# Split weights of the feed-forward stage in idle big tiles, and adding loads at other places

## The chip, the cores and the metric

The kernel runs on one core of a Trainium2 chip. The metric is the device time of one execution in microseconds (us). Three runs of the kernel before gave 1895.63, 1897.59 and 1898.46 us; their median is 1897.59.

## The reference

One layer of a decoder trunk for 256 tokens, model width 2048, all in 32-bit floats: three parallel mixers, then a gated feed-forward stage, then a per-layer embedding, and a final norm. The change lies in the feed-forward stage (D_FF = 5632).

```python
merged = (jax.nn.sigmoid(m_a) * u_a + jax.nn.sigmoid(m_b) * u_b
          + jax.nn.sigmoid(m_c) * u_c)
x = x + merged @ w_o[i]
h = rms_norm(x, g_ffn[i])
gate, up = jnp.split(h @ w_gate_up[i], 2, axis=-1)
x = x + (jax.nn.silu(gate) * up) @ w_down[i]
x = x + (p[i] @ w_ple[i]) * jax.nn.sigmoid(rms_norm(x, g_ple[i]) @ w_ple_gate[i])
return rms_norm(x, g_final)
```

## The kernel before

TensorE multiplies 32-bit data as a sum of three products of rounded parts. Each weight W is split into whi, W rounded to TensorE's 32-bit input format, and wlo = W - whi; the activations are split too. `three` (L242 to L246) issues the three matmuls, 128x128 by 128x512 each: L244 with whi, L245 with wlo, L246 with whi again.

The feed-forward stage runs from about 1058 us on. Gate and up are made in 11 blocks of 512 columns each (`Quad`, j = 0 to 10), and after the blocks 0 to 2, 3 to 5, 6 to 8 and 9 to 10 come four down groups of 512 output columns each, which use the results of these blocks. Blocks up to the next down groups are called a batch. A block has eight places; each place takes one pair of loads (a gate load and an up load of 512 KB, 128 partitions x 2 x 512) and is of kind "s" or "o" by the string "soosooso". In an "s" pair VectorE also makes sums of the two loads (L236, L276), so that seven products do the work of eight (21 matmuls, with four pieces of split weight). An "o" pair has two pieces and 24 matmuls. A block has 3 x 21 + 5 x 24 = 183 matmuls.

What is done to one load, in order:

- SyncE loads it into one of six raw buffers (L152).
- ScalarE copies it with rounding into whi (L216).
- Then wlo is made in one of two ways. By subtraction: VectorE takes raw - whi (L228). Or by an **adding load**: ScalarE writes -whi into wlo (L220), and a DMA that GpSimd (POOL) issues (L221) fetches the weight once more from memory and adds it there. An adding load takes no time of VectorE and lets the raw buffer go as soon as whi is made.

Before the change the up load of each "o" pair is done with an adding load, five per block; in block 0, which takes the pairs in the order 1, 2, 0, 4, 3, 5, 6, 7, only at places from 4 on (`START`'s second number), which are two "o" pairs, at places 5 and 7. That makes 2 + 10 x 5 = 52.

whi and wlo lie in seven buffers each (`PARTS`), and `room` lets a piece be split only when fewer than seven are in use. A pool of 13 big tiles (128 partitions x 8 x 256 floats) holds the residual stream (two), the split activations (eight) and aT, the transposed results of a batch's blocks (three); a tile for aT is taken when its block's result is transposed, so of the three some are idle until then.

The order of all instructions is fixed when the program is built. `Flow` keeps a model clock for ScalarE and VectorE, with a time for a load to land, a gap between loads, and a time for an adding load; `fill` emits, ahead of each matmul step, the splits and evictions that fit before it by that clock. On the chip each engine takes its queue in this order, and waits for its operands by semaphores. The evictions in question are `quad_mid` (gate part: L1332 on ScalarE, L506 on VectorE), the sigmoids of the result (L1345, ScalarE, with a load of the function table ahead of them), the transposes (L1287 on TensorE) with their copies into aT (L515, L516), and `ev_down` (L506 into xr, on VectorE).

Of the kernel before, what the change touches and what calls it, by code (L numbers as in the profile page):

```python
# [11 lines left out]
F32R = mybir.dt.float32r  # L12
# [7 lines left out]
P = 128  # L20
T = 256
D = 2048
NB = 512
# [17 lines left out]
class Group:  # L41
# [6 lines left out]
    def __init__(self, w, kts, c0, n, stat, evac, need=(), pre=None, kind="tok", cost=1.3, key=None):  # L48
        self.w, self.kts, self.c0, self.n = w, list(kts), c0, n
        self.stat, self.evac, self.need, self.pre, self.kind = stat, evac, need, pre, kind  # L50
        self.cost, self.key = cost, key
        self.ps = None
        self.held = []
# [9 lines left out]
class Quad:  # L63
# [6 lines left out]

    def __init__(self, w, c0, c1, pairs, mid, end, order=None, plain=0):
        self.w, self.cs, self.pairs, self.mid, self.end = w, (c0, c1), pairs, mid, end
        self.order = list(order or range(len(pairs)))
        self.plain = plain
        self.ps = {}


# [14 lines left out]
class Piece:  # L94


    def __init__(self, n):
        self.n = n
        self.ops = []
        self.parts = []  # L100
        self.left = 0
# [12 lines left out]
class Flow:  # L114


    RAWS, PARTS = 6, 7
    LAND, GAP, ADDED = 5.0, 1.3, 8.0

    def __init__(self, nc, tc, pools, nm, big, split, quad_parts):  # L120
# [33 lines left out]

    def room(self, piece):
        self.live = [p for p in self.live if p.left]
        return sum(p.n for p in self.live) + piece.n <= self.PARTS

    def next_split(self):

# [10 lines left out]
    def do_split(self, op):  # L171
        if op.piece is not None and op.piece not in self.live:
            p = op.piece
            for part in ("whi", "wlo"):
                p.parts.append([
                    self.pools["wparts"].tile([P, 2, NB], F32R, tag=part, name=self.nm(part)) for _ in range(p.n)
                ])
            self.live.append(p)
        self.emit(self.todo.pop(0))
        for z in op.frees:  # L180
            z.freed = True
            self.slots.append(op.end)
        self.issue()
# [70 lines left out]
    def add_quad(self, g):  # L254
# [2 lines left out]
        first_p, last_p = g.order[0], g.order[-1]  # L257
        for pos, p in enumerate(g.order):
            kind = g.pairs[p]
            r1, r2 = (Load(g.w, 2 * p, c, NB) for c in g.cs)  # L260
            if kind == "s":
                self.loads += [r2, r1]
                pc = [Piece(1) for _ in range(4)]
                x = []

                def new_sum(x=x):
# [9 lines left out]
                        self.nc.vector.tensor_tensor(out=X(0), in0=R2(0), in1=R2(1), op=ALU.add),  # L276
                    ), [], r2,
                )
                b1 = self.split_ops(pc[0], 0, lambda r=r1: r.raw, load=r1)
                t1 = self.add_op(lambda R2=R2: R2(0), lambda R2=R2: R2(0), lambda R1=R1: R1(0), [t3], r1)  # L280
                t2 = self.add_op(lambda X=X: X(1), lambda R2=R2: R2(0), lambda R2=R2: R2(1), [t1], r1)
                self.split_ops(pc[1], 0, lambda r=r2: r.raw, [t1], r2, [r2])
# [15 lines left out]
                              after=(lambda g=g: self.late(g.mid(g, g.ps), g)) if p == last_s and z == "4" else None)  # L298
            else:
                self.loads += [r2, r1]  # L300
                pc = [Piece(1) for _ in range(2)]
                self.split_ops(pc[1], 0, lambda r=r2: r.raw, load=r2, frees=[r2],
                               neg=None if pos < g.plain else g.w[:, 2 * p : 2 * p + 2, g.cs[1] : g.cs[1] + NB])
                self.split_ops(pc[0], 0, lambda r=r1: r.raw, load=r1, frees=[r1])
# [156 lines left out]
def kernel(  # L461
# [284 lines left out]
    w_in_v, w_gu_v, w_dn_v = wv(w_in), wv(w_gate_up), wv(w_down)  # L746
# [513 lines left out]
    PAIRS = "soosooso"  # L1260
# [163 lines left out]
        return f  # L1424

    NJ = 11
    START = ((1, 2, 0, 4, 3, 5, 6, 7), 4)
    flow.transposes(None, [x_part(3, j) for j in (0, 2)])
    plan = []
    for lo, hi in ((0, 3), (3, 6), (6, 9), (9, NJ)):  # L1430
        for j in range(lo, hi):
            plan.append(Quad(w_gu_v, j * NB, (NJ + j) * NB, PAIRS, quad_mid, quad_end(j), *(START if j == 0 else ())))
        for c in range(4):
            plan.append(Group(w_dn_v, range(4 * lo, 4 * hi), c * NB, NB, blk(aT), ev_down(c, hi == NJ), key="a"))

# [146 lines left out]
```

## Time and profile before

| | us |
|---|---|
| median of three runs | 1897.59 |
| the profiled execution | 1896.41 |
| its span (first to last instruction) | 1894.6 |
| TensorE busy in the span | 1867.9 |
| VectorE busy | 1320.2 |
| ScalarE busy | 1041.1 |
| feed-forward stage's 52 adding loads: median from issue to landing | 8.2 |

The profile is of one execution. Its page gives the busy time of each engine and the costliest groups of instructions; a group's row has the line of the kernel, the engine, the output and inputs by tile, the number of instructions, their busy time and mean in ns, and the idle time ahead of them with what ended it. The timeline gives single instructions: start and duration in us, engine, line, operation, and in brackets the idle time before it and what ended that. Names as in the code: whi and wlo are the split weights, st the split activations, acc an accumulator of TensorE, xr the residual stream, ga, vx and gs the gate's intermediate results. A matmul of 128x512 reads 0.39 us long in a timeline since matmuls overlap; start to start they are 0.227 us apart.

### The profile page before, as it was taken

Reading aid. Unit: us, or ns where it says so; the run is one execution under the profiler, and the core shown is the slowest. Engines: PE = TensorE matmul, PEld = TensorE weight load, DVE = VectorE, ACT = ScalarE, POOL = GpSimd, SP = SyncE. Lnnn points to the kernel's source line nnn. Section 1 sums busy time; section 2 is a strip of 40 time slices with the busy share of each in tenths; the row PEclk is TensorE's granted clock in tenths of the full one; section 3 lists DMA queues with packets and bytes.
Section 4 is the critical chain, followed back from the end, with each engine's and each line's share of the span. In section 5 each row is a group of like instructions: output and inputs, shape, how many; then the busy total and the mean of one; then the engine's idle time right before and its main releaser. Section 6 shows DMA issues by size and latency. Waiting matters only on the chain.

```text
span 1894.6 us, 23186 instructions
## 1 busy us (share of the span) xinstructions
PE 1867.9 (99%) x8589; PEld 1551.7 (82%) x8589; DVE 1320.2 (70%) x1657; ACT 1041.1 (55%) x1204; POOL 71.7 (4%) x74
## 2 busy tenths in 40 slices
PE   8999999999999999999999999999999999999997
PEld 6888888888888888888888778888888888887887
DVE  6457777668888889655556777758765776676654
ACT  6656556554454435644445666546644665465654
POOL 0000000000000000000000011001100110010000
PEclk9999999999999999999999999999999999999999
DMA  8766556556666656676655599679976997698552
GB/s 311 238 181 186 176 177 190 168 154 178 190 186 193 194 160 211 198 236 189 188 189 167 194 255 263 222 199 259 268 228 192 250 263 239 187 252 277 178 161 95
DMA packets 204401, 390.47 MB, mean 206 GB/s; under 512 B 12432, under 2 KB 21264, under 8 KB 203904
## 3 DMA queue, kind: packets, MB, share of 16 engines
q1 hardware_dynamic: 189248, 358.12, 59.5%
q0 software_dynamic: 15040, 30.87, 9.3%
q8 instruction: 67, 1.10, 0.2%
q14 instruction: 46, 0.38, 0.1%
HBM read 386.85 MB, written 2.10 MB: 205 GB/s over the span
## 4 chain that ended last, share of the span: by engine, by line
PE 92%; DMA 3%; DVE 3%; ACT 1%; issue 1%; SPq 0%; DVEq 0%; ACTq 0%
PE acc L651 17%; PE acc L652 17%; PE acc L650 17%; PE acc L246 12%; PE acc L245 12%; PE acc L244 12%; DMA wlo<-in_w_gate_up_dram 1%; DMA raw<-in_w_gate_up_dram 1%; DVE wlo L228 1%; PE tr L719 1%; PE tr L1287 1%; PE sc L928 1%; DMA x<-in_x_feat_dram 0%; DMA pt<-in_p_feat_dram 0%; DVE raw L236 0%
## 5 line engine op out<-in xcount | busy, mean ns | idle before, releaser
L516 DVE TENSOR_TENSOR wlo<-raw,whi 128x1024 fp32r<-128x1024 f32 (+2 forms) x378 | 450.0, 1196 | 293.9 <-ACT whi L515 293.3
L515 ACT ACTIVATE whi<-raw 128x1024 fp32r<-128x1024 f32 (+2 forms) x378 | 391.2, 1037 | 465.1 <-PE acc L652 391.8
L216 ACT ACTIVATE whi<-raw 128x1024 fp32r<-128x1024 f32 (+1 forms) x333 | 332.3, 1006 | 301.4 <-PE acc L246 267.0
L650 PE MATMUL acc<-whi,hhi 128*128 128x512 f32 (+1 forms) x1120 | 432.7, 387 | 5.5 <-ACT whi L515 5.5
L651 PE MATMUL acc<-wlo,hhi 128*128 128x512 f32 (+1 forms) x1120 | 430.1, 384 | 0.5 <-DVE wlo L516 0.5
L652 PE MATMUL acc<-whi,hlo 128*128 128x512 f32 (+1 forms) x1120 | 430.1, 384 | 0.0
L228 DVE TENSOR_TENSOR wlo<-raw,whi 128x1024 fp32r<-128x1024 f32 (+1 forms) x281 | 318.1, 1144 | 155.6 <-ACT whi L216 154.7
L245 PE MATMUL acc<-wlo,st 128*128 128x512 f32 x671 | 262.1, 391 | 4.1 <-DMA wlo<-in_w_gate_up_dram 3.6
L244 PE MATMUL acc<-whi,st 128*128 128x512 f32 x671 | 262.0, 393 | 1.6 <-DVE xr L506 1.5
L246 PE MATMUL acc<-whi,st 128*128 128x512 f32 x671 | 261.5, 391 | 0.0
L650 PEld LDWEIGHTS acc<-whi,hhi 128*128 128x128 f32 x1120 | 210.8, 188 | 46.5 <-ACT whi L515 5.9
L651 PEld LDWEIGHTS acc<-wlo,hhi 128*128 128x128 f32 x1120 | 210.9, 188 | 41.9 <-DVE wlo L516 1.4
L652 PEld LDWEIGHTS acc<-whi,hlo 128*128 128x128 f32 x1120 | 210.7, 188 | 41.3
L245 PEld LDWEIGHTS acc<-wlo,st 128*128 128x128 f32 x671 | 126.3, 188 | 32.0 <-DMA wlo<-in_w_gate_up_dram 5.0
L244 PEld LDWEIGHTS acc<-whi,st 128*128 128x128 f32 x671 | 126.3, 188 | 29.1 <-DVE xr L506 1.5
L246 PEld LDWEIGHTS acc<-whi,st 128*128 128x128 f32 x671 | 126.4, 188 | 26.4
L244 PE MATMUL acc<-whi,aT 128*128 128x512 f32 x352 | 138.3, 393 | 1.5 <-ACT aT L515 1.5
L245 PE MATMUL acc<-wlo,aT 128*128 128x512 f32 x352 | 137.2, 390 | 0.0
L246 PE MATMUL acc<-whi,aT 128*128 128x512 f32 x352 | 136.6, 390 | 0.0
L509 DVE SCALAR_TENSOR_TENSOR cv<-uT,vec,cv 128x255 f32<-128x255 f32 (+15 forms) x240 | 110.8, 466 | 4.8
L221 POOL DMA_DIRECT2D wlo<-in_w_gate_up_dram x52 | 62.6, 1204 | 819.9 <-ACT wlo L220 485.8
L244 PEld LDWEIGHTS acc<-whi,aT 128*128 128x128 f32 x352 | 66.2, 188 | 15.5 <-ACT aT L515 2.1
(276 smaller groups left out, 2073.7 us busy)
## 6 DMA issues: line engine op xcount, KB each, us to landing
raw<-in_w_in_dram SPq DMA_DIRECT2D x262, 512.0 KB, 3.7
raw<-in_w_gate_up_dram SPq DMA_DIRECT2D x176, 512.0 KB, 5.3
raw<-in_w_down_dram SPq DMA_DIRECT2D x88, 512.0 KB, 5.1
wlo<-in_w_gate_up_dram POOLq DMA_DIRECT2D x52, 512.0 KB, 8.2
raw<-in_w_gla_out_dram SPq DMA_DIRECT2D x32, 512.0 KB, 3.6
raw<-in_w_o_dram SPq DMA_DIRECT2D x32, 512.0 KB, 4.0
raw<-in_w_ple_gate_dram SPq DMA_DIRECT2D x24, 512.0 KB, 3.6
raw<-in_w_sc_out_dram SPq DMA_DIRECT2D x16, 512.0 KB, 4.3
```

The source lines that it names most:

```text
L216: a = self._op("A", cost * 0.88, lambda: nc.scalar.activation(out=hi(), in_=src(), func=AF.Copy), deps, load, piece, frees if neg else ())
L221: nc.gpsimd.dma_start(out=lo(), in_=neg, accum_op=ALU.add)
L228: lambda: nc.vector.tensor_tensor(out=lo(), in0=src(), in1=hi().bitcast(F32), op=ALU.subtract),
L244: pe.matmul(o, lhsT=s[0], rhs=w[0], start=start, stop=False)
L245: pe.matmul(o, lhsT=s[0], rhs=w[1], start=False, stop=False)
L246: pe.matmul(o, lhsT=s[1], rhs=w[0], start=False, stop=stop)
L509: dve.scalar_tensor_tensor(out=o, in0=a, scalar=s, in1=b, op0=op0, op1=op1)
L515: a = act.activation(out=hi, in_=src, func=AF.Copy)
L516: b = dve.tensor_tensor(out=lo, in0=src, in1=hi.bitcast(F32), op=ALU.subtract)
L650: pe.matmul(o, lhsT=shi[:, hs], rhs=whi, start=st, stop=False)
L651: pe.matmul(o, lhsT=shi[:, hs], rhs=wlo, start=False, stop=False)
L652: pe.matmul(o, lhsT=slo[:, hs], rhs=whi, start=False, stop=sp)
```

## The change

It has three parts, all in the planning of the gate and up blocks:

- `START`'s second number goes from 4 to 8, so block 0 has no adding load; the up loads at its places 5 and 7 are split by VectorE's subtraction.
- `NEG = (0,)`: in the ten blocks after it the gate load of the "s" pair at place 0 is done with an adding load too: six per block, 60 in all.
- A piece may have a count `may`. Where the seven ordinary buffers are taken, such a piece is split into a big tile instead ("wp": both whi and wlo lie in one), as long as fewer than `may` pieces lie in big tiles. `may` is lo + 3 - j, the number of aT tiles not yet taken when block j's work starts: 3, 2 and 1 in the three blocks of a batch, 3 and 2 in the last batch's two; in the first block of a batch only places from 2 on have it.

```diff
@@ class Flow
     RAWS, PARTS = 6, 7
+    NEG = (0,)
     LAND, GAP, ADDED = 5.0, 1.3, 8.0
...
     def room(self, piece):
         self.live = [p for p in self.live if p.left]
-        return sum(p.n for p in self.live) + piece.n <= self.PARTS
+        return self.held(False) + piece.n <= self.PARTS or self.held(True) < piece.may
+
+    def held(self, extra):
+        return sum(p.n for p in self.live if p.extra == extra)
...
     def do_split(self, op):
         if op.piece is not None and op.piece not in self.live:
             p = op.piece
-            for part in ("whi", "wlo"):
-                p.parts.append([
-                    self.pools["wparts"].tile([P, 2, NB], F32R, tag=part, name=self.nm(part)) for _ in range(p.n)
-                ])
+            p.extra = self.held(False) + p.n > self.PARTS
+            if p.extra:
+                b = self.big("wp", (P, 2, 2, NB), F32R)
+                p.parts = [[b[:, 0, :, :]], [b[:, 1, :, :]]]
+            else:
+                for part in ("whi", "wlo"):
...
             kind = g.pairs[p]
+            may = g.spare if pos > 1 or g.spare < 3 else 0
             r1, r2 = (Load(g.w, 2 * p, c, NB) for c in g.cs)
             if kind == "s":
                 self.loads += [r2, r1]
-                pc = [Piece(1) for _ in range(4)]
+                pc = [Piece(1, may) for _ in range(4)]
...
-                b1 = self.split_ops(pc[0], 0, lambda r=r1: r.raw, load=r1)
+                b1 = self.split_ops(pc[0], 0, lambda r=r1: r.raw, load=r1,
+                                    neg=g.w[:, 2 * p : 2 * p + 2, g.cs[0] : g.cs[0] + NB] if pos in self.NEG and not g.plain else None)
...
-    START = ((1, 2, 0, 4, 3, 5, 6, 7), 4)
+    START = ((1, 2, 0, 4, 3, 5, 6, 7), 8)
...
-            plan.append(Quad(w_gu_v, j * NB, (NJ + j) * NB, PAIRS, quad_mid, quad_end(j), *(START if j == 0 else ())))
+            plan.append(Quad(w_gu_v, j * NB, (NJ + j) * NB, PAIRS, quad_mid, quad_end(j), *(START if j == 0 else (None, 0)), lo + 3 - j))
```

Since the planner's clock sees other costs, the order on the engines moves. All lines of the changed kernel stand 11 to 13 lines lower (L216 is L227, L220 is L231, L221 is L232, L228 is L239, L236 is L247, L276 is L288, L506 is L519, L515 is L528, L1332 is L1345, L1345 is L1358). The first number behind a tile's name is the tile's own.

VectorE in block 0, where place 4's subtractions end, before (wlo_1512, the up load of place 5, isn't there: it is an adding load; wlo_1515 is the gate load's, the next ones belong to place 6):

```order
L228 TENSOR_TENSOR wlo_1515_8547<-raw_1491_8450,whi_1514_8546 128x1024
L236 TENSOR_TENSOR raw_1494_8456<-raw_1494_8456,raw_1499_8470 128x512
L228 TENSOR_TENSOR wlo_1519_8564<-raw_1499_8470,whi_1518_8563 128x1024
L236 TENSOR_TENSOR sum_1517_8561<-raw_1494_8456 128x512
L228 TENSOR_TENSOR wlo_1521_8582<-raw_1494_8456,whi_1520_8581 128x1024
L236 TENSOR_TENSOR raw_1499_8470<-raw_1499_8470,sum_1517_8561 128x512
L228 TENSOR_TENSOR wlo_1524_8601<-sum_1517_8561,whi_1523_8600 128x1024
```

and with the change:

```order
L239 TENSOR_TENSOR wlo_1512_8534<-raw_1485_8435,whi_1511_8533 128x1024
L239 TENSOR_TENSOR wlo_1515_8543<-raw_1491_8450,whi_1514_8542 128x1024
L288 TENSOR_TENSOR sum_1517_8557<-raw_1494_8456 128x512
L239 TENSOR_TENSOR wlo_1519_8560<-raw_1499_8470,whi_1518_8559 128x1024
L247 TENSOR_TENSOR raw_1494_8456<-raw_1494_8456,raw_1499_8470 128x512
L247 TENSOR_TENSOR sum_1517_8557<-raw_1494_8456 128x512
L247 TENSOR_TENSOR raw_1499_8470<-raw_1499_8470,sum_1517_8557 128x512
L239 TENSOR_TENSOR wlo_1521_8581<-raw_1494_8456,whi_1520_8580 128x1024
L239 TENSOR_TENSOR wlo_1524_8594<-sum_1517_8557,whi_1523_8593 128x1024
```

The subtraction of wlo_1512 stands ahead of the rest, which follows behind it; the first sum (L276, now L288), which stood ahead of these rows, comes behind the two subtractions.

ScalarE at the end of block 0 and the start of block 1, before (whi_1535 to whi_1546 belong to place 0 of block 1, whi_1554 and wlo_1555 to the up load of its place 1, ga and gs to block 0's result):

```order
L216 ACTIVATE whi_1535_8640<-raw_1516_8553 128x1024
L216 ACTIVATE whi_1539_8660<-raw_1513_8536 128x1024
L1332 ACTIVATE ga_1538_8658<-acc_1498_8465 128x512
L216 ACTIVATE whi_1543_8698<-sum_1534_8638 128x1024
L216 ACTIVATE whi_1546_8714<-raw_1516_8553 128x512
L216 ACTIVATE whi_1554_8740<-raw_1522_8591 128x1024
L220 ACTIVATE wlo_1555_8741<-whi_1554_8740 128x1024
L1345 ACT_TABLE_LOAD
L1345 ACTIVATE gs_1541_8669<-ga_1538_8658,y_1445_8278 128x512 x2
L216 ACTIVATE whi_1557_8747<-raw_1527_8608 128x1024
```

and with the change (the two rows ahead are whi_1535 and its negated copy, wlo_1536):

```order
L1345 ACTIVATE ga_1541_8664<-acc_1498_8465 128x512
L227 ACTIVATE whi_1537_8651<-raw_1513_8540 128x1024
L227 ACTIVATE whi_1543_8691<-sum_1534_8636 128x1024
L227 ACTIVATE whi_1546_8713<-raw_1516_8549 128x512
L227 ACTIVATE whi_1554_8739<-raw_1522_8584 128x1024
L1358 ACT_TABLE_LOAD
L1358 ACTIVATE gs_1542_8671<-ga_1541_8664,y_1445_8278 128x512 x2
L231 ACTIVATE wlo_1555_8740<-whi_1554_8739 128x1024
L227 ACTIVATE whi_1557_8746<-raw_1527_8613 128x1024
```

The negated copy of wlo_1555, which its adding load waits for, has moved from ahead of the table load and the sigmoids to behind them.

ScalarE where the down groups end and block 6 begins, before (whi_2079 to whi_2088 are place 0 of block 6, whi_2091 the up load of its place 1):

```order
L216 ACTIVATE whi_2079_11336<-raw_2065_11248 128x1024
L216 ACTIVATE whi_2083_11358<-raw_2060_11226 128x1024
L216 ACTIVATE whi_2086_11377<-sum_2078_11322 128x1024
L216 ACTIVATE whi_2088_11393<-raw_2065_11248 128x512
L216 ACTIVATE whi_2091_11411<-raw_2068_11266 128x1024
L220 ACTIVATE wlo_2092_11412<-whi_2091_11411 128x1024
L216 ACTIVATE whi_2094_11430<-raw_2071_11284 128x1024
```

and with the change (whi_2068 to whi_2077 are place 0, whi_2080 is the up load of place 1, the wp tiles belong to place 2):

```order
L231 ACTIVATE wlo_2069_11329<-whi_2068_11328 128x1024
L227 ACTIVATE whi_2072_11351<-raw_2049_11218 128x1024
L227 ACTIVATE whi_2075_11370<-sum_2067_11314 128x1024
L227 ACTIVATE wp_2086_11429<-raw_2063_11294 128x1024
L231 ACTIVATE wp_2086_11429<-wp_2086_11429 128x1024
L227 ACTIVATE whi_2077_11386<-raw_2054_11240 128x512
L227 ACTIVATE whi_2080_11404<-raw_2057_11258 128x1024
L227 ACTIVATE wp_2088_11435<-raw_2066_11312 128x1024
L231 ACTIVATE wlo_2081_11405<-whi_2080_11404 128x1024
L227 ACTIVATE whi_2083_11423<-raw_2060_11276 128x1024
```

The splits of place 2, with a negated copy, stand ahead of the last split of place 0 and of place 1's own.

More of the change, by code (lines that the diff above doesn't have):

```diff
@@ L63, with __init__ @@
 class Quad:
-    def __init__(self, w, c0, c1, pairs, mid, end, order=None, plain=0):
+    def __init__(self, w, c0, c1, pairs, mid, end, order=None, plain=0, spare=0):
         self.w, self.cs, self.pairs, self.mid, self.end = w, (c0, c1), pairs, mid, end
@@ L76, in __init__ @@
         self.plain = plain
+        self.spare = spare
         self.ps = {}
@@ L94, with __init__ @@
 class Piece:
-    def __init__(self, n):
+    def __init__(self, n, may=0):
         self.n = n
+        self.may, self.extra = may, False
         self.ops = []
@@ L173, in do_split @@
             p = op.piece
-            for part in ("whi", "wlo"):
-                p.parts.append([
-                    self.pools["wparts"].tile([P, 2, NB], F32R, tag=part, name=self.nm(part)) for _ in range(p.n)
-                ])
+            p.extra = self.held(False) + p.n > self.PARTS
[4 more added lines that the diff above has]
+                for part in ("whi", "wlo"):
+                    p.parts.append([
+                        self.pools["wparts"].tile([P, 2, NB], F32R, tag=part, name=self.nm(part)) for _ in range(p.n)
+                    ])
             self.live.append(p)
@@ L300, in add_quad @@
                 self.loads += [r2, r1]
-                pc = [Piece(1) for _ in range(2)]
+                pc = [Piece(1, may) for _ in range(2)]
                 self.split_ops(pc[1], 0, lambda r=r2: r.raw, load=r2, frees=[r2],
```

## The prediction

> **What bounds the kernel now.** I read the page first: engines, then the costliest groups.
>
> ```profile
> PE 1867.9 (99%) x8589; PEld 1551.7 (82%) x8589; DVE 1320.2 (70%) x1657; ACT 1041.1 (55%) x1204; POOL 71.7 (4%) x74
> ...
> L221 POOL DMA_DIRECT2D wlo<-in_w_gate_up_dram x52 | 62.6, 1204 | 819.9 <-ACT wlo L220 485.8
> ```
>
> TensorE is busy 99% of the span and the change adds or removes no matmul, so only its waits can move the time, and all waits together are about 27 us (1894.6 - 1867.9). The change touches the feed-forward stage alone; the view of waits, for TensorE between 1058 and 1742 us, says what is there to win:
>
> ```profile
> PE acc L245 <- DMA wlo<-in_w_gate_up_dram: 3.6, 2, 3.2
> PE acc L244 <- DVE xr L506: 1.5, 3, 0.9
> ```
>
> The columns are the total, the number of waits and the longest. Nearly everything is one wait of 3.2 us for an adding load. The timeline of TensorE shows it and what comes behind it:
>
> ```profile
> 1089.84 0.39 PE L246 MATMUL acc<-whi,st 128*128 128x512 f32 x1
> ...
> 1090.75 0.39 PE L244 MATMUL acc<-whi,st 128*128 128x512 f32 x1
> 1094.32 0.50 PE L245 MATMUL acc<-wlo,st 128*128 128x512 f32 x1 [3.19 <-DMA wlo<-in_w_gate_up_dram]
> ...
> 1096.39 0.63 PE L245 MATMUL acc<-wlo,st 128*128 128x512 f32 x1
> 1096.82 0.63 PE L246 MATMUL acc<-whi,st 128*128 128x512 f32 x1
> ...
> 1098.52 0.42 PE L244 MATMUL acc<-whi,st 128*128 128x512 f32 x1
> 1098.78 0.39 PE L245 MATMUL acc<-wlo,st 128*128 128x512 f32 x1
> ```
>
> Undisturbed starts are 0.227 us apart (four steps lie between the first two rows; a block of 183 matmuls is some 42 us). The next step takes 3.57, which is 3.34 too much. Then matmuls start 0.43 apart: from 1094.32 to 1098.78 there are 12 steps in 4.46 us, where 12 x 0.227 = 2.72 would do, 1.74 too much. The windows name the cause, a granted clock of about half:
>
> ```profile
> 1060.00:1090.00 30.00, 29.41 (x130) 23.67 (x131) 29.54 (x44) 24.05 (x33) 1.24 (x1) 1.00 0.66 206
> 1095.00:1098.60 3.60, 3.60 (x11) 2.77 (x10) 0.00 (x0) 0.00 (x0) 0.00 (x0) 0.53 1.08 379
> ```
>
> (after the engines' busy times: clock, DMA share, GB/s.) The stall thus costs 3.34 + 1.74 = **5.1 us**.
>
> **The change part by part.** *1. Block 0 has no adding load.* The awaited one is that of the pair at place 5:
>
> ```profile
> 1084.10 1.04 ACT L220 ACTIVATE wlo<-whi 128x1024 fp32r<-128x1024 f32 x1
> ...
> 1085.44 1.24 POOL L221 DMA_DIRECT2D wlo<-in_w_gate_up_dram  x1 [246.97 <-DMA raw<-in_w_gate_up_dram]
> ...
> DMA to landing us min/median/max: 8.8/8.8/8.8
> ```
>
> (The last line is the view of L221 in a window that holds this DMA alone.) It lands at 1085.44 + 8.8 = 1094.3; TensorE wanted it at 1090.98. Instead VectorE subtracts, at the place of the rows
>
> ```profile
> 1083.23 0.68 DVE L228 TENSOR_TENSOR wlo<-raw,whi 128x512 fp32r<-128x512 f32 x1
> 1083.83 0.68 DVE L276 TENSOR_TENSOR sum<-raw 128x512 f32<-128x512 f32 x1
> 1084.43 1.22 DVE L228 TENSOR_TENSOR wlo<-raw,whi 128x1024 fp32r<-128x1024 f32 x1
> 1085.57 0.68 DVE L236 TENSOR_TENSOR raw<-raw,raw 128x512 f32<-128x512 f32 x1
> ...
> 1089.65 1.22 DVE L228 TENSOR_TENSOR wlo<-sum,whi 128x1024 fp32r<-128x1024 f32 x1
> ```
>
> so from 1083.83 to about 1085.0, six us early. VectorE is full here (29.54 of 30 us, above), so everything behind slides by one spacing of 1.14 us (1085.57 - 1084.43). Late next would be the residual of the sum at place 6: done at 1090.87 before, now about 1092.0, and wanted 12 matmuls after 1090.98, at 1093.7: 1.7 us of cover. The price if that is gone is what exceeds it. I take the whole 5.1 as gained; bounds 3.4 (the 1.7 given back) and 5.1.
>
> *2. Block 1's second adding load comes late.* Before, its negated copy stands ahead of a table load and two sigmoids on ScalarE; now it stands behind them, and a negated copy for the new adding load of place 0 stands ahead of the whole run.
>
> ```profile
> 1098.75 1.06 ACT L216 ACTIVATE whi<-raw 128x1024 fp32r<-128x1024 f32 x1 [5.45 <-PE acc L246]
> ...
> 1102.84 1.75 ACT L216 ACTIVATE whi<-raw 128x512 fp32r<-128x512 f32 x2 [0.23 <-PE acc L246]
> 1104.62 1.06 ACT L220 ACTIVATE wlo<-whi 128x1024 fp32r<-128x1024 f32 x1
> 1105.70 1.28 ACT L1345 ACT_TABLE_LOAD   x1
> 1106.99 1.34 ACT L1345 ACTIVATE gs<-ga,y 128x512 f32<-128x512 f32 x2
> ...
> 1105.98 1.20 POOL L221 DMA_DIRECT2D wlo<-in_w_gate_up_dram  x1 [11.16 <-ACT wlo L220]
> ...
> DMA to landing us min/median/max: 9.1/9.1/9.1
> ...
> 1116.93 0.39 PE L245 MATMUL acc<-wlo,st 128*128 128x512 f32 x1
> ```
>
> Before: issued at 1105.98, landed at 1115.1, used at 1116.93 (last row). With the stall gone the use moves to 1116.93 - 5.1 = 1111.8. ScalarE's run from 1098.75 to 1104.59 is 5.84 long; it is released by TensorE, so it starts at 1093.65 and has one more negated copy: 1093.65 + 5.84 + 1.06 = 1100.6 at the earliest. Followed wait by wait (each split waits for a buffer that TensorE frees) I get 1101.8. Then table load 1.28, sigmoids 1.34, negated copy 1.06, 0.3 to the issue: 1104.6 to 1105.8. Landing after 8.2 (the median of all, below) to 9.1: 1112.8 to 1114.9, so a wait of 1.0 to 3.1 us. By the later issue and the 8.8 of the neighbour it lands at 1114.6, 2.8 late; I take **2.6**. No half clock behind it: 3.19 idle was followed by one; the second longest wait of this stage (0.9) was not, and between them the trace has nothing there. Cost if it comes: up to 1.74.
>
> By the Trainium skill (TensorE: Matmul & The Clock Gate, Why this matters for your kernels) idle gaps of TensorE should stay under about 3 us, since one idle window brings the half clock back. The 3.19 us above agree; 2.6 would be under it, 3.1 over it, and by the rule the sum would be 1.74 smaller only in that upper case.
>
> *3. Ten more adding loads at place 0 of blocks 1 to 10* (52 - 2 + 10 = 60 in all). Each takes a subtraction of 1.14 from VectorE and gives ScalarE a copy of 1.06 and POOL an issue of 1.2; POOL is 4% busy. Time to landing, from the view of L221 over the stage:
>
> ```profile
> DMA to landing us min/median/max: 5.9/8.2/9.9
> ```
>
> The order of instructions gives the room: between the matmul that frees the buffer and the first use stand 53 matmuls in blocks 1 and 2 and at least 71 from block 3 on, x 0.227 = 12.0 and 16.1 us. Two copies and two hand-overs of 0.3 take 2.7 of it, which leaves 9.3 and 13.4 for the DMA. Against 8.2 to 9.9 that loses 0 to 0.6 in each of blocks 1 and 2, nothing later; I take 0.2 in all.
>
> *4. Splits in big tiles* (blocks 3 to 10) let a split run before one of the seven ordinary buffers is free. In block 8 this wait should go, since 79 matmuls instead of 55 stand between release and use (5.4 us more); block 2's smaller one too (67 instead of 55):
>
> ```profile
> 1553.34 0.50 PE L245 MATMUL acc<-wlo,st 128*128 128x512 f32 x1 [0.42 <-DMA wlo<-in_w_gate_up_dram]
> ```
>
> That is 3.6 - 3.2 = 0.4 gained; bounds 0 and 0.4. At the starts of blocks 3, 6 and 9 TensorE waits 1.5 in all for an eviction that stands behind subtractions on VectorE:
>
> ```profile
> 1453.07 1.22 DVE L228 TENSOR_TENSOR wlo<-raw,whi 128x1024 fp32r<-128x1024 f32 x1
> 1454.21 1.28 DVE L506 TENSOR_TENSOR xr<-xr,acc 128x512 f32<-128x512 f32 x2
> ...
> 1455.03 0.47 PE L244 MATMUL acc<-whi,st 128*128 128x512 f32 x1 [0.87 <-DVE xr L506]
> ```
>
> A raw slot is freed earlier there (gain at most 1.5), but by the order ScalarE makes a big-tile half and a negated copy, 2 x 1.06, ahead of the half that this subtraction needs; if one of them isn't covered at each start, 3 x 1.06 = 3.2 is lost. I take 0.
>
> *5. DMA engines.* From the queues
>
> ```profile
> q1 hardware_dynamic: 189248, 358.12, 59.5%
> q0 software_dynamic: 15040, 30.87, 9.3%
> ...
> 1106.30:1148.70 42.40, 42.40 (x193) 35.12 (x192) 34.03 (x43) 30.24 (x34) 5.96 (x6) 1.00 0.95 260
> 1148.70:1191.50 42.80, 42.71 (x192) 35.05 (x191) 31.84 (x38) 28.83 (x31) 5.72 (x5) 1.00 0.98 270
> 1200.00:1250.00 50.00, 50.00 (x226) 41.40 (x225) 30.90 (x32) 20.26 (x21) 0.00 (x0) 1.00 0.57 180
> ```
>
> a plain load of 0.524 MB takes 0.595 x 1894.6 / 358.12 x 0.524 = 1.65 us of all 16 engines, an adding one 0.093 x 1894.6 / 30.87 x 0.524 = 3.0. A block with five adds needs 16 x 1.65 + 5 x 3.0 = 41.4 of 42.4 us, which the shares 0.95 and 0.98 bear out; with six 44.4, a share of 1.05. Short stretches ran at 1.08 (above), and the down groups at 0.57 let the six raw buffers fill ahead. Taken as 0; the other end is a rival.
>
> **Sum:** -5.1 + 2.6 + 0.2 - 0.4 = **-2.7 us**. Against the profiled execution's own 1896.41 (span 1894.6 and 1.8 around it) that is 1893.7; this execution lies 1.2 under the median of 1897.59, and on the median the forecast is **1894.9**.
>
> **The rivals.** *No new wait in block 1*: the adding load lands by 1111.8. For it: landings down to 5.9 exist, and 6.0 after the later issue would do. Against: the neighbours in this stretch took 8.8 and 9.1. -5.1 - 0.4 + 0.2 = -5.3, or -6.8 with the 1.5 of the starts: 1890.8 to 1892.3. *Half clock again*: the wait passes 3 us and brings the 1.74 too: -2.7 + 0.5 + 1.74 = -0.5, 1897.1. *The DMA engines are oversubscribed* (the slower side): place, blocks 1 to 10; price 44.4 - 42.4 = 2.0 us per block if a sustained share cannot exceed 1.0; it decides once the lead of the raw loads is used up. Batches have 2, 3, 3 and 2 such blocks, 20 us; a lead of 3 us per batch (half a raw load's landing time, an estimate) leaves 8: 1894.9 + 8 = 1903. For it: 0.98 already. Against: no TensorE wait for a raw load or its split behind 0.98, and stretches at 1.08. The Trainium skill (DMA: Bandwidth & Descriptors, Issuing engines are not separate DMA queues) says that DMAs of all issuers interleave on the same 16 engines; the 0.98 with both queues agrees, so POOL's queue gives no room of its own. *The change does nothing net*: place 0's loads and the starts give back all, about 1897.6.
>
> **How the numbers follow.** Forecast 0.50 (1893.0 to 1896.5), no new wait 0.22, half clock again 0.13, oversubscribed 0.09, nothing net 0.06. The range 1890.8 to 1899.0 leaves out most of the oversubscribed case and the tails. 0.2% is 3.8 us, about what a measurement of this kernel can tell from no change. Faster by more (under 1893.8): all of the second case and a third of the first, 0.38; slower by more (over 1901.4): 0.07; within: 0.55.
>
> **What would show it.** Right: no wait at the last matmuls of block 0 and clock 1.00 there; one wait of 1 to 3 us for an adding load at block 1's place 1, its issue right behind two sigmoids; no wait there over 0.6 at place 0. Wrong: waits for adding loads or splits spread over blocks 3 to 10 with DMA shares over 1.0 and times to landing over 10 us; evictions of xr over 1 us late; a wait in block 0 for VectorE.

## The result, and the profile after

The changed kernel takes 1914.31 us (median of four runs, 1913.0 to 1915.3) against 1896.61 for the kernel before in the same comparison: a ratio of 1.0086, 95% interval 1.0074 to 1.0099. It is slower by 17 us, where 2.7 us less were forecast. The profiled execution took 1913.0 us, with a span of 1911.2.

The page's engines and its group of adding loads into ordinary buffers (ten more go into big tiles, in a group of their own):

```profile
PE 1872.7 (98%) x8589; PEld 1553.0 (81%) x8589; DVE 1312.4 (69%) x1649; ACT 1043.4 (55%) x1212; POOL 81.4 (4%) x82
...
L232 POOL DMA_DIRECT2D wlo<-in_w_gate_up_dram x50 | 60.2, 1204 | 768.8 <-ACT wlo L231 680.7
```

TensorE has the same 8589 matmuls. All waits are now 38.5 us (1911.2 - 1872.7) instead of 26.7. The view of waits, TensorE in the feed-forward stage, says on what:

```profile
PE acc L255 <- DVE vx L519: 14.4, 7, 3.9
PE acc L255 <- DVE ga L519: 1.8, 1, 1.8
PE acc L255 <- ACT aT L528: 1.1, 1, 1.1
PE acc L256 <- DMA wlo<-in_w_gate_up_dram: 0.4, 1, 0.4
```

The row for adding loads fell from 3.6 to 0.4, and the row for xr, 1.5 before, is gone. In their place stand eight waits for the evictions of the gate's accumulators (vx, ga), a row that was not there before. All lie at the ends of blocks 3, 4, 6, 7 and 9: the blocks of batches 2 to 4 that are followed by another block. In the trace these are also the only batches with pieces in big tiles. In start-to-start time of TensorE over 0.227 us, with two half clocks of 6.83 us, they lose 6.7, 3.7, 8.5, 2.1 and 3.4 us, **24.3** together; the whole stage loses 29.6 where it lost 14.1.

VectorE at the end of block 3 before the change, where the four evictions (L506) stand together and the next block's sum (L276) comes behind them:

```profile
1298.04 0.68 DVE L506 TENSOR_TENSOR vx<-acc,ga 128x512 f32<-128x512 f32 x1
1298.76 0.69 DVE L506 TENSOR_TENSOR vx<-vx,acc 128x512 f32<-128x512 f32 x1
1299.36 0.68 DVE L506 TENSOR_TENSOR ga<-ga,acc 128x512 f32<-128x512 f32 x1
1299.96 0.69 DVE L506 TENSOR_TENSOR ga<-acc,vx 128x512 f32<-128x512 f32 x1
1300.78 0.69 DVE L276 TENSOR_TENSOR sum<-raw 128x512 f32<-128x512 f32 x1
```

The timeline of TensorE and of VectorE there with the change (brackets: idle before, and what ended it):

```profile
1299.50 0.39 PE L257 MATMUL acc<-whi,st 128*128 128x512 f32 x1
1303.40 0.79 PE L255 MATMUL acc<-whi,st 128*128 128x512 f32 x1 [3.52 <-DVE vx L519]
1303.99 0.63 PE L256 MATMUL acc<-wlo,st 128*128 128x512 f32 x1
```

```profile
1290.47 0.69 DVE L288 TENSOR_TENSOR sum<-raw 128x512 f32<-128x512 f32 x1 [3.87 <-DMA raw<-in_w_gate_up_dram]
1291.08 0.69 DVE L239 TENSOR_TENSOR wlo<-raw,whi 128x512 fp32r<-128x512 f32 x1
1291.69 0.68 DVE L519 TENSOR_TENSOR vx<-acc,ga 128x512 f32<-128x512 f32 x1
1292.40 0.69 DVE L519 TENSOR_TENSOR vx<-vx,acc 128x512 f32<-128x512 f32 x1
1296.07 0.69 DVE L247 TENSOR_TENSOR raw<-raw,raw 128x512 f32<-128x512 f32 x1 [2.98 <-DMA raw<-in_w_gate_up_dram]
1296.68 1.22 DVE L239 TENSOR_TENSOR wp<-raw,wp 128x1024 fp32r<-128x1024 f32 x1
1297.81 0.68 DVE L519 TENSOR_TENSOR ga<-ga,acc 128x512 f32<-128x512 f32 x1
1298.41 0.68 DVE L247 TENSOR_TENSOR sum<-raw 128x512 f32<-128x512 f32 x1
1299.01 0.68 DVE L519 TENSOR_TENSOR ga<-acc,vx 128x512 f32<-128x512 f32 x1
```

The rows with L519 are the evictions. Between the second and the third stands a sum (L247) of the two raw loads of place 3 of the *next* block; it waits there 2.98 us for a load, and the remaining evictions, which free the accumulators that block 4 starts on, wait behind it. The two waits on loads are in series: the first sum (1290.47) holds up the half-sized subtraction behind it, which frees a raw buffer (by the ring of six, the one that the second load goes into), so SyncE issues the second load only at 1291.80, and it lands at 1296.04. The DMA view of 20 us around it, in slices of 0.5 us, shows the pause:

```profile
DMA  4945999999999999999400000973899999999999
GB/s 160 98 61 147 319 295 258 258 201 209 201 205 205 201 209 254 266 311 381 168 4 0 0 0 0 53 53 90 209 324 344 221 205 213 250 262 258 356 315 266
```

From 1290 to 1292.5 almost nothing moves, although over the whole stretch from 1257 to 1299.5 us the DMA engines are busy 0.97 of the time. Between two issues of raw loads (1235 to 1740 us) the trace of before has no pause over 6 us; after has eleven, seven of them over 7.

The instructions carry numbers in the order in which the planner recorded them. The two evictions are 10244 and 10262, the sum is 10310: the planner recorded it behind them, and the scheduler that builds the program moved it ahead, presumably as ready by its own times for a load (its reason is not shown).

### The profile page after: what moved, and what is told of

The parts are those of the page before. It is cut to its first block, busy times and chain, and to the rows that moved or that the text cites. A ratio compares the mean times of both kernels' runs of the same rounds, so it can differ in the third digit from the quotient of the medians.

```text
span 1911.2 us, 23231 instructions
## 1 busy us (share of the span) xinstructions
PE 1872.7 (98%) x8589; PEld 1553.0 (81%) x8589; DVE 1312.4 (69%) x1649; ACT 1043.4 (55%) x1212; POOL 81.4 (4%) x82
## 4 chain that ended last, share of the span: by engine, by line
PE 89%; DMA 4%; DVE 4%; issue 2%; ACT 1%; SPq 0%; POOL 0%; DVEq 0%; ACTq 0%; POOLq 0%
PE acc L664 17%; PE acc L665 17%; PE acc L663 17%; PE acc L255 11%; PE acc L256 11%; PE acc L257 11%; DMA raw<-in_w_gate_up_dram 2%; DVE wlo L239 1%; DMA wlo<-in_w_gate_up_dram 1%; PE tr L732 1%; PE tr L1300 1%; PE sc L941 1%; ACT whi L227 1%; DVE vx L519 0%; DVE ga L522 0%
## 5 line engine op out<-in xcount | busy, mean ns | idle before, releaser
L528 ACT ACTIVATE whi<-raw 128x1024 fp32r<-128x1024 f32 (+2 forms) x378 | 391.1, 1037 | 464.3 <-PE acc L665 389.9
L227 ACT ACTIVATE whi<-raw 128x1024 fp32r<-128x1024 f32 (+1 forms) x302 | 298.8, 1002 | 267.2 <-PE acc L257 216.1
L239 DVE TENSOR_TENSOR wlo<-raw,whi 128x1024 fp32r<-128x1024 f32 (+1 forms) x252 | 286.0, 1142 | 158.0 <-ACT whi L227 157.1
L255 PE MATMUL acc<-whi,st 128*128 128x512 f32 x578 | 228.2, 397 | 16.4 <-DVE vx L519 14.4
L256 PE MATMUL acc<-wlo,st 128*128 128x512 f32 x578 | 226.6, 393 | 0.9 <-DMA wlo<-in_w_gate_up_dram 0.4
L257 PE MATMUL acc<-whi,st 128*128 128x512 f32 x578 | 226.1, 392 | 0.0
L255 PEld LDWEIGHTS acc<-whi,st 128*128 128x128 f32 x578 | 109.2, 189 | 43.1 <-DVE vx L519 18.1
L256 PEld LDWEIGHTS acc<-wlo,st 128*128 128x128 f32 x578 | 109.4, 189 | 24.4 <-DMA wlo<-in_w_gate_up_dram 1.3
L257 PEld LDWEIGHTS acc<-whi,st 128*128 128x128 f32 x578 | 109.4, 189 | 23.1
L232 POOL DMA_DIRECT2D wlo<-in_w_gate_up_dram x50 | 60.2, 1204 | 768.8 <-ACT wlo L231 680.7
```

Source lines behind the costliest of these rows:

```text
L227: a = self._op("A", cost * 0.88, lambda: nc.scalar.activation(out=hi(), in_=src(), func=AF.Copy), deps, load, piece, frees if neg else ())
L232: nc.gpsimd.dma_start(out=lo(), in_=neg, accum_op=ALU.add)
L239: lambda: nc.vector.tensor_tensor(out=lo(), in0=src(), in1=hi().bitcast(F32), op=ALU.subtract),
L255: pe.matmul(o, lhsT=s[0], rhs=w[0], start=start, stop=False)
L256: pe.matmul(o, lhsT=s[0], rhs=w[1], start=False, stop=False)
L257: pe.matmul(o, lhsT=s[1], rhs=w[0], start=False, stop=stop)
```

## The experiments

Theory B, formed from this trace: the order on VectorE costs the time; the big tiles let sums of the next block stand ahead of evictions, and on the chip they wait there for loads. Theory A: the traffic of the adding loads makes loads late, and the order only shows it. Ratios are to the kernel before.

**The parts of the change.** `e1_start` keeps the first part alone, `e2_start_neg` the first two, `e3_start_spare` the first and third.

```diff
 e1, e3:
-    NEG = (0,)
+    NEG = ()
 e1, e2:
-    ... (None, 0)), lo + 3 - j))
+    ... (None, 0)), 0))
```

> Only the first part of the change: block 0 without adding loads; no adding load at place 0, no splits in big tiles (50 adding loads). Both theories: the stall of block 0 with its half clock goes, 5.1 us less than before, 4 to 5.5 with the slide of VectorE's queue; no wait of TensorE over 1 us at the block ends.

> The first and second part: block 0 without adding loads, six adding loads in each later block (60), no splits in big tiles. Queue-order theory (sums of the next block, which the big tiles let in early, stand ahead of the block-end evictions in VectorE's queue and wait there for a raw load): no waits for vx or ga at block ends, 2 to 5 us less than before. Traffic theory (the eight more adding loads fill the DMA engines and make raw loads late): the waits of the changed kernel are here too, 8 to 17 us more than before.

> The first and third part: block 0 without adding loads, five in each later block (50), splits in big tiles as in the changed kernel. Queue-order theory: the block-end waits for vx and ga are all here, 10 to 18 us more than before. Traffic theory: with two adding loads fewer than before they are gone, 3 to 5 us less than before.

Measured: e1 1898.23 us (1.0006, 0.9998 to 1.0015), e2 1895.52 (0.9992, 0.9984 to 1.0001), e3 1904.07 (1.0037, 1.0025 to 1.0049).

- e1 missed: block 0's 5.1 us went, but block 1 loses 7.3 instead. Its first two adding loads are issued back to back, behind two sigmoids and five copies, and TensorE waits 5.4 us for the first. ScalarE, then GpSimd, then the view of L232 in a window with these two:

```profile
1103.00 4.41 ACT L227 ACTIVATE whi<-raw 128x512 fp32r<-128x512 f32 x5
1107.32 1.99 ACT L231 ACTIVATE wlo<-whi 128x1024 fp32r<-128x1024 f32 x2
```

```profile
1108.67 2.48 POOL L232 DMA_DIRECT2D wlo<-in_w_gate_up_dram  x2 [270.12 <-DVE ga L522]
```

```profile
DMA to landing us min/median/max: 9.7/11.2/12.8
```

- e2 has 60 adding loads and no wait for vx or ga: the traffic alone does not bring them. It is 1.5 us under before, where the queue-order theory had 2 to 5. The rest of its gain goes at the three batch starts, where TensorE waits for xr, 4.8 us and a half clock, 7.2 in all.
- e3 has 50 adding loads, fewer than before, and waits for vx of 7.8 us at the same five block ends, some 12 lost with what follows them. (Block 1 loses here as in e1, so e1 is the base to set it against.) It is 7 us over before, and neither theory had that: one expected 10 to 18 more, the other 3 to 5 less. So the big tiles bring the waits; they cost 5.8 us with five adding loads (e3 - e1) and 18.8 with six (1914.3 - e2). Both theories have a part in that.

**The order alone.** `e10_keep` records the same instructions as the changed kernel, and forbids a split or sum on VectorE to be moved ahead of an eviction recorded before it.

```diff
+        if op.eng == "D" and op.split and ev is not None:
+            with self.tc.issue_after(ev):
+                op.fn()
+        else:
+            ins = op.fn()
+            if op.eng == "D" and not op.split:
+                self.ev = ins or ev
```

> The whole change, 60 adding loads and the same pieces in big tiles, recorded in the same order; one thing is added: a split or sum on VectorE that is recorded behind an eviction may not be moved ahead of it. Queue-order theory: the block-end waits of 23 us in all (3.7, 2.2, 1.1, 2.0, 4.1, 0.6, 1.1, 2.8 and two half clocks) go, down to 3 us at most, and the kernel is 3 to 7 us faster than before. Traffic theory: the raw loads are as late as they were, and most of the waits stay, over 8 us more than before.

Measured: 1915.2 us (1.0111, 1.0094 to 1.0128; two of its six runs took 1921 and 1924). The waits for vx and ga are gone, as theory B had it, and the time is not. TensorE's waits are now

```profile
PE acc L265 <- DMA wlo<-in_w_gate_up_dram: 16.6, 5, 4.9
```

on adding loads: one of 4.9 in block 1, which the rule brings there, the others around the ends of blocks 4 and 7 and in the blocks behind them. What is late are the raw loads under them: 22 of the 126 of batches 2 to 4 take over 9 us to land, and there are twelve pauses over 7 us (eleven and seven in the changed kernel). Some of this is the rule's own work, as the run with the sums alone shows below. The same rule on the first two parts, `f5_neg_keep`:

> The first two parts of the change (60 adding loads, no big tiles), with the rule that no split or sum on VectorE moves ahead of an eviction that is recorded before it. Without the rule the three batch starts cost 7.2 us (waits for xr of 4.8 and a half clock), since the eviction stands behind a sum that waits for a raw load. Theory B: these waits fall under 1.5 us in all, 4 to 6 us less than the 1895.5 without the rule. Theory A: the loads are as late, the waits go over to the matmuls that use them; no more than 2 us less.

Measured: 1904.71 us (1.0032, 1.0021 to 1.0042), 9 more than e2, so theory B's 4 to 6 less fell. The waits for xr stay (5.4 us), and one of 5.5 for an adding load in block 1 is new. The rule holds back subtractions too, and with them raw buffers.

**Fewer adding loads.** `f1_three_spare` and `f2_three_plain` have three adding loads in each later block, with and without big tiles.

```diff
-  neg=None if pos < g.plain else ...
+  neg=None if pos < g.plain or pos in (2, 5) else ...
```

> Splits in big tiles as in the changed kernel, no adding load in block 0, and only three adding loads in each later block (places 1, 4, 7), 30 in all. A block then needs 16 x 1.65 + 3 x 3.0 = 35.4 of 42.4 us of the DMA engines. To be set against the same kernel without big tiles (next run): with five adding loads the big tiles cost 5.8 us, with six 18.8. Theory A (loads come late only because the DMA engines are near their limit, and the big tiles bunch them): no cost here, under 2 us over the next run, no block-end waits for vx. Theory B (the order on VectorE alone, two landings in series ahead of an eviction): still 4 us or more over the next run, with waits for vx at the ends of blocks 3, 4, 6, 7 and 9.

> The same 30 adding loads without splits in big tiles: the base of the run before. VectorE makes 22 subtractions more than with 50 adding loads (25 us over ten blocks that have 8 us of idle VectorE each), so both theories expect it within 3 us of the 1898 of the kernel with 50, and no waits at block ends.

Measured: 1900.72 (1.0012, 1.0002 to 1.0022) and 1897.23 (0.9995, 0.9986 to 1.0004). The big tiles cost 3.5 us here, between the two expectations; waits for vx are there (3.3 us, at the ends of blocks 3, 6 and 9), and no raw load takes over 9 us. So the order costs some even where the DMA engines have time to spare (an estimated 35.4 of 42.4 us needed). The cost grows with the traffic: 3.5, 5.8 and 18.8 us with three, five and six adding loads, with none, six and eleven raw loads over 9 us in the runs with big tiles. The planner's order changes along with it, so these runs don't tell how much of the growth is the traffic's alone.

**The planner's landing time.** It says when a split is recorded. `f4_land9` alters one number of the changed kernel, and `h3_land9_again` repeats it.

```diff
-    LAND, GAP, ADDED = 5.0, 1.3, 8.0
+    LAND, GAP, ADDED = 9.0, 1.3, 8.0
```

> The whole change, with one number of the planner altered: it takes 9.0 us instead of 5.0 for a raw load to land. It then puts 24 instead of 31 pieces in big tiles and records the splits later. Theory A: the traffic is the same, bunched somewhat less; still 8 us or more over before. Theory B: fewer sums stand between the evictions of a block's end (one instead of two at most), so the waits for vx fall to less than half of the 14.4 us, and the kernel is 0 to 6 us over before.

> The whole change with the planner's landing time at 9.0, once more, on this chip: 1892.7 before. Expected again within 2 us of it, 3 to 6 us less than the kernel before.

Measured: 1892.65 us (0.9968, 0.9956 to 0.9980) and 1892.59 (0.9971, 0.9962 to 0.9980). The number turns the change from 17 us slower into 5 us faster, more than theory B expected. Waits of TensorE in the stage, f4:

```profile
PE acc L255 <- DVE vx L519: 2.2, 4, 1.3
PE acc L256 <- DVE wlo L239: 0.4, 1, 0.4
PE tr L1300 <- DVE xr L519: 0.4, 1, 0.4
PE acc L256 <- DMA wlo<-in_w_gate_up_dram: 0.3, 1, 0.3
```

and VectorE at the end of block 3:

```profile
1297.44 1.22 DVE L239 TENSOR_TENSOR wlo<-raw,whi 128x1024 fp32r<-128x1024 f32 x1
1298.58 0.68 DVE L519 TENSOR_TENSOR ga<-ga,acc 128x512 f32<-128x512 f32 x1
1299.17 0.68 DVE L519 TENSOR_TENSOR ga<-acc,vx 128x512 f32<-128x512 f32 x1
1300.69 0.69 DVE L247 TENSOR_TENSOR raw<-raw,raw 128x512 f32<-128x512 f32 x1 [0.83 <-DMA raw<-in_w_gate_up_dram]
```

The sum waits for its load here too. The load lands at 1300.66, after 8.7 us and 0.9 us ahead of block 4's first matmul (1.0 in the changed kernel), but the third and fourth evictions stand ahead of the sum, and TensorE has only 0.7 us of loss there. The landings are no better than in the changed kernel: of the loads issued from 1235 to 1740 us the median is 5.57 us against 5.56, and eleven take over 9 us in both. With as many adding loads and the same landing times the waits are nearly gone. What differs is the order of the queues, and with it the times of issue: there are three pauses over 7 us instead of seven.

The number without the change (`g1_before_l9`), and without the big tiles (`g2_neg_l9`):

> The kernel before with the planner's landing time at 9.0 instead of 5.0, nothing else. Theory B (order on VectorE; the buffers' number, not the landing time, held the sums back in the kernel before): the number decides little without big tiles, within 3 us of before, block 0's 5 us stall stays or moves to block 1. Rival (9.0 is a gain of its own, the change adds nothing to it): 4 us or more less than before.

> First and second part of the change with the landing time at 9.0, no big tiles. It tells what the big tiles are worth once the order is right: the whole change with 9.0 took 1892.7. Theory B: the waits for xr at the three batch starts (7.2 us without big tiles at 5.0) stay in part, 1 to 4 us more than 1892.7. Rival: big tiles are worth nothing, within 1 us of 1892.7.

Measured: 1897.41 us (0.9992, 0.9984 to 1.0001) and 1899.3 (1.0005, 0.9996 to 1.0014). The number does nothing clear of noise for the kernel before. With it the big tiles are worth 6.7 us (1899.3 - 1892.6, from two comparisons whose kernels before differ by 0.7), more than the 1 to 4 that theory B expected; without them waits for xr of 6.2 us stay at the batch starts.

Other values, `g3_land8` (8.0) and `g4_land10` (10.0):

> The whole change with the landing time at 8.0. The order on VectorE at the ends of blocks 3, 6 and 9 is then still the changed kernel's (sum of two raw loads and a big-tile subtraction ahead of the third eviction), at the ends of blocks 4 and 7 a sum stands ahead of the third eviction but one subtraction fewer ahead of the fourth. Theory B: losses at the ends of 3, 6 and 9 as in the changed kernel (18 us with half clocks; at least 8), less at 4 and 7; in all 6 to 16 us more than before. Rival (the cost falls evenly with the number of pieces in big tiles, 29 of 31 here, 24 at 9.0): the time would lie about a third of the way from 1914.3 to 1892.7 and losses would be spread over all block ends alike.

> The whole change with the landing time at 10.0: 15 pieces in big tiles, and between the evictions of a block's end at most one sum. Theory B: no block-end wait over 1.5 us; within 2 us of the 1892.7 at 9.0, so at least 2 us less than before. Rival (fewer pieces in big tiles, less gain): between 1892.7 and before, no wait over 1.5 us either.

Measured: 1915.49 us (1.0088, 1.0071 to 1.0106) and 1929.09 (1.0158, 1.0144 to 1.0172). At 8.0, with 29 pieces in big tiles and the sum still ahead of the third eviction, the ends of blocks 3, 6 and 9 lose 19.6 us with their half clocks: a step with the order, as theory B has it, not a third of the way; the whole is 17 us over before, where theory B had 6 to 16. At 10.0 both expectations fell. ScalarE shows why:

```profile
1284.25 1.06 ACT L227 ACTIVATE wp<-raw 128x1024 fp32r<-128x1024 f32 x1 [11.58 <-DMA raw<-in_w_gate_up_dram]
1285.21 1.04 ACT L227 ACTIVATE whi<-raw 128x1024 fp32r<-128x1024 f32 x1
```

A copy into a big tile stands at the head of its queue and waits for a load that took 11.8 us; whatever stands behind it waits too, no raw buffer is freed, and no raw load is issued for 17.1 us (1272.37 to 1289.43). It is the same mechanism on another engine, at another place.

**The sums alone.** `h2_two_evictions` narrows e10's rule on the changed kernel: only sums, and only against the third and fourth eviction. GpSimd and SyncE keep the changed kernel's order. ScalarE and TensorE do not quite, other than expected: at the block ends some instructions change places with near neighbours (behind block 3 a split into a big tile comes ahead of the negated copy that it followed). `h4_land9_two` sets the rule on the 9.0 us order.

```diff
+        if op.eng == "D" and op.split and op.cost < 0.64 and ev is not None:
...
+            if op.key:
+                self.ev = ins or ev
```

> The whole change with one order altered, on VectorE alone: a sum (lines L288 and L247) that is recorded after the two evictions of the gate's third and fourth accumulator at a block's end may not be moved ahead of them. Subtractions keep their places, ScalarE, TensorE, GpSimd and SyncE theirs. Theory B (these sums, waiting there for a raw load, cost the time): the waits for vx and ga at the ends of blocks 3, 4, 6, 7 and 9 (16.2 us) fall under 4 us and the kernel is within 5 us of before or faster. Theory A2 (the raw loads themselves are late because they are issued in bunches; an order that serves the evictions only moves the wait, as in the run with the rule for all splits): the time stays over 1907, with waits for adding loads in place of those for vx.

> The landing time at 9.0 and the rule of the first run of this set together. Theory B: the rule takes away the small waits for vx left at 9.0 (2.2 us), 0 to 2 us less than 9.0 alone. Theory A2: moving the sums back makes the loads behind them late, 5 us or more over 9.0 alone.

Measured: 1907.63 us (1.0054, 1.0041 to 1.0067) and 1902.27 (1.0027, 1.0017 to 1.0037). In h2 the waits for vx and ga at the five block ends are gone; TensorE's waits in the stage are

```profile
PE acc L265 <- DMA wlo<-in_w_gate_up_dram: 8.1, 4, 4.0
PE acc L264 <- DVE vx L528: 2.3, 1, 2.3
```

(the 2.3 at the end of block 0, where the rule costs 4.1 with a half clock). It is 6.7 us less than the changed kernel and still 10 over before: moving the sums wins a part, and the rest comes back as adding loads that are late around the ends of blocks 4 and 7 (5.0 and 6.7 lost), with ten pauses over 7 us. The time is what theory A2 expected (raw loads late because they come in bunches), at its border of 1907. But the trace shows that at least one of these pauses comes from the order too. At the end of block 3 the second load of the sum lands at 1296.14, and the sum runs only at 1306.82, without a wait:

```profile
1298.90 0.69 DVE L528 TENSOR_TENSOR ga<-acc,vx 128x512 f32<-128x512 f32 x1 [0.67 <-PE acc L266]
...
1306.82 0.69 DVE L256 TENSOR_TENSOR raw<-raw,raw 128x512 f32<-128x512 f32 x1
```

Under the rule most of the gate's remaining work stands between the last of the four evictions and the sum. The next raw load is issued at 1310.12, when a subtraction behind the sum has ended, 8.7 us after the one before it. In e10 it is the same: the load lands at 1299.32, the sum runs at 1308.98, and the pause is 8.8 us. So both runs put the sums too far back instead of just behind the evictions, and neither is a clean test of the order against the traffic. On the 9.0 us order the rule costs 9.7 us, all in batch 1, most of it one wait of 6.0 for an adding load in block 2.

**More raw buffers.** `i1_raws8` gives the changed kernel eight raw buffers and six ordinary ones for split weights, in the same memory; `i2_raws8_plain` is that without big tiles.

```diff
-    RAWS, PARTS = 6, 7
+    RAWS, PARTS = 8, 6
```

> The whole change with eight raw buffers instead of six and six ordinary buffers for split weights instead of seven (the same memory); landing time 5.0, 43 pieces in big tiles. Theory A2 (with big tiles the splits run ahead of what six raw buffers can feed; a split that waits for a load holds the buffers behind it, so the loads pause and then come in bunches): two more loads in flight, the pauses over 7 us between two issues (7 in the changed kernel, none before) go to 2 or fewer, the block-end losses of 24 us to under 8, and the kernel is within 4 us of before or faster. Theory C (six adding loads are too much traffic once splits run ahead, however many raw buffers): waits stay, over 1905.

> Eight raw buffers and six for split weights without big tiles, 60 adding loads: the base of the run before. Six ordinary buffers give each adding load two buffers' less lead at most (a matmul step of 2.7 us each), so waits for adding loads come: both theories expect it slower than the 1895.5 with seven and six, by 3 to 30 us, and under theory A2 slower than the run before.

Measured: 1908.38 us (1.0051, 1.0039 to 1.0063) and 1914.23 (1.0081, 1.0067 to 1.0096). With eight raw buffers (and six ordinary ones) the big tiles gain 5.9 us, where with six (and seven) they cost 18.8, although more pieces use them (43 instead of 31). In i1 no matmul waits for vx or ga:

```profile
PE acc L256 <- DMA wlo<-in_w_gate_up_dram: 14.1, 9, 3.4
PE acc L256 <- DVE wlo L239: 0.5, 1, 0.5
PE tr L1300 <- DVE xr L519: 0.4, 1, 0.4
```

The time is 10 us over before and missed the 4 us that theory A2 expected: some 12 of its 26 us are lost in blocks 0 to 2, which have no big tiles and now only six ordinary buffers, and some 11 in batches 2 to 4; three pauses over 7 us are left. Theory C (too much traffic, however many raw buffers) expected over 1905 with waits, and that is what came; as a rule it falls with f4, which carries the same 60 adding loads in 1892.6 us.

## Why the prediction was wrong

- *The stall of block 0*: right. TensorE has no loss there and no half clock; the term of 5.1 holds.
- *Block 1's second adding load, 2.6 us late*: mis-sized. Its issue came at 1105.73 (1104.6 to 1105.8 were forecast), from behind the sigmoids as the order said, but the DMA view has a landing of 5.9 us for it, not 8.2 to 9.1:

```profile
1105.73 1.21 POOL L232 DMA_DIRECT2D wlo<-in_w_gate_up_dram  x1 [8.19 <-ACT wlo L231]
...
DMA to landing us min/median/max: 5.9/5.9/5.9
```

  It landed at 1111.6, just in time for 1111.8; this is the rival "no new wait in block 1", whose total came out wrong all the same. Place 0's load landed at 1104.48, 8.2 us after its issue, as forecast. The wait of 0.05 us that block 1 has is a third load's.
- *Place 0's loads in later blocks, and blocks 2 and 8*: right within 0.5 us. One adding load after block 4 waits 0.4.
- *The batch starts, taken as 0*: they gained. TensorE's waits for xr there (1.5) are gone.
- *Splits in big tiles*: **the step that failed.** Its working looked at what big tiles free (waits for buffers) and at the batch starts, where evictions were known to stand behind splits. It did not read VectorE's order at the other block ends, where before the evictions stand together, and with the change a sum stands between them. The room that it counted for the adding loads was right and did not bear on this: the wait is not for an adding load but for a raw load, in front of an eviction. Beside the 0.4 above, the prediction put this part of the change at 0 (its lower end a gain of 1.5, its upper end 3.2 lost at the batch starts); the five block ends lose 24.3 us. With these and 2 gained at the batch starts, and the 0.2 and 0.4 left as forecast, the sum is -5.1 + 0.2 - 0.4 - 2.0 + 24.3 = 17.0. Measured is 17.7 between the medians, 16.6 between the two profiled executions.
- *The DMA engines, taken as 0*, with the argument that six raw buffers fill ahead in the down groups. The slower rival had the side but not the mechanism: its price was a rate (2.0 us per block), its sign late loads everywhere. e2 carries the same traffic without those waits, and f4 with the same landings is, with its repeat, the fastest of all. With more traffic the slow landings become more, so that an instruction placed too early waits longer; the cost with three, five and six adding loads fits this, but does not part it from the order.

In all: big tiles let splits and sums be recorded, and moved, further ahead than six raw buffers can feed, while the planner counts on a landing time of 5.0 us; the median is 5.6, and 15 of 125 take over 8.7. A sum that waits on VectorE holds the evictions behind it, and holds the subtraction that frees the next raw buffer, so that loads pause and then come in bunches that land later still. That the big tiles bring the loss is shown by the pairs with and without them, and that the order which the planner and the scheduler make decides its size by f4 and g3 (24 and 29 pieces, ten or eleven landings over 9 us in both, 23 us apart). No run isolates the sum ahead of the evictions: the two rules that moved it changed more than that, and got back 6.7 us at most. That the pauses come from the raw buffers is supported by i1 and i2, in which the sign of the big tiles' worth turns, but not isolated, since the ordinary buffers changed with them. No rule was found for why 9.0 gives a good order and 8.0 and 10.0 bad ones; that 9.0 was tried first among them is luck.

The version that beats both is the change with the landing time at 9.0: 1892.6 us, 0.3% less than before in two sets of runs.

## What to carry to other kernels

When a change lets work run further ahead, read the order of each in-order queue at the places where something else must get through, evictions above all: an instruction that waits there for a transfer makes all behind it as late as the transfer. Where buffers no longer hold the work back, a planner's time for a transfer decides that order, and its value has to be tried: here 9.0 us was 5 us better than before, and 8.0 and 10.0 were 17 and 31 worse. And a stall that is taken away in one place is worth its time only if what the next block needs comes earlier with it: e1 removed 5.1 us, but the first adding load of block 1 was issued at 1108.67 instead of 1105.98, and 7.3 us were lost some twenty us later.

## What the runs showed of the hardware

The half clock does not follow from the longest wait alone. f4 has it for 3.41 us from 1153.38, 1.8 us after the end of a wait of 1.31 (and one of 0.30 between):

```profile
1151.56 0.50 PE L255 MATMUL acc<-whi,st 128*128 128x512 f32 x1 [1.31 <-DVE vx L519]
...
1153.39 0.63 PE L257 MATMUL acc<-whi,st 128*128 128x512 f32 x1
```

while the changed kernel waits 2.63 us at block 9's end and runs on at full clock:

```profile
1709.22 0.50 PE L255 MATMUL acc<-whi,st 128*128 128x512 f32 x1 [2.63 <-DVE vx L519]
1709.56 0.40 PE L256 MATMUL acc<-wlo,st 128*128 128x512 f32 x1
```

Inside the feed-forward stage its length was always 3.41 or 6.83 us. The Trainium skill (TensorE: Matmul & The Clock Gate, Part 1: The HAM clock gate) has a free-running window of about 3.4 us; the lengths agree with one and two of them. The Trainium skill's advice on the same page of no idle gaps over about 3 us (Why this matters for your kernels) is too wide a bound here: 1.31 us, with 0.30 behind it, was enough once, and 2.63 was not another time.

A raw load of 512 KB took up to 15.3 us to land (in e10), and longer the more loads were under way: there six raw loads were issued between 1312.3 and 1318.7, with an adding load among them, and took 3.5, 5.3, 6.3, 9.2, 11.2 and 12.0 us in this order.
